# An ordering pass learns that VectorE and GpSimd take turns, and looks 500 instructions ahead instead of 300

## The chip, the cores and the metric

One core of one Trainium2 chip. The metric is device time in microseconds (us) from a launch's start to its end, as the median of several runs. The kernel before takes 2632.96 us (median of 3 runs, 2631.53 to 2633.64). Five engines work at once: TensorE (PE in the profile), VectorE (DVE), ScalarE (ACT), GpSimd (POOL), and SyncE (SP), which here issues every DMA. Each engine takes its instructions strictly in the order of its own queue; an instruction whose operands aren't ready holds up all those behind it on that engine, and no others, until someone waits for one of them.

## The reference

One layer of a bidirectional encoder over two sequences, one of 512 tokens and one of 1024, model width 1024, all in float32:

```python
h = rms_norm(x, n_pre_mix)
proj = h @ w_in                                   # 1024 x 6672
# Gated DeltaNet, 4 heads, forward and backward in time:
qkv = silu(centred_dwconv(qkv_g, conv_w))         # 5 taps
a_mat = where(strict, (k*beta) @ k.T * decay, 0)  # per chunk of 64
sol = triangular_solve(I + a_mat, [v*beta, k*beta*exp(cum)])
o_a = scan over chunks of (q, k, u, w, state)
# HGRN2, 4 heads, forward and backward: a linear recurrence with a decay per channel
o_b = gla_chunked(qh, kh, ih, logf)
merged = sigmoid(gate0) * (norm(o_a)*silu(z) @ w_br_gdn) + sigmoid(gate1) * (norm(o_b)*silu(g) @ w_br_hg)
x = x + rms_norm(merged @ w_out)
y = x + rms_norm((silu(h2 @ w_gate) * (h2 @ w_up)) @ w_down)   # d_ff 2816
```

## The kernel before, in words

The kernel is not written in the order in which it runs. `layer` calls its operations on a `Tape`, which only records them (about 19,400 operations, numbered in the order of recording); a simple planner, `Plan`, weaves the streams of work (`gdn_stream`, `hg_stream`, `pre_stream`, `dense_stream`, `p2_stream`) into that recording. Then `Tape.schedule` puts the operations into their final order and `Tape.emit` writes them out. Nearly every instruction therefore carries the one line number of `emit`: 564 before, 577 in the changed kernel, which has 13 lines more above it. In the profile groups are told apart by tile names instead: `la_a`, `ba_a`, `xa_a`, `da_a` and `xr_a` are large SBUF areas of 512-column buffers, `ha_a` holds the normalised activations, `wa_a` the split weights, `sm_a` and `sa_a` small tiles, `bank` is PSUM.

`schedule` is a list scheduler. It holds a clock for each engine and, for every operation, a duration (`o.dur`) and the time for which it occupies its engine (`o.occ`), both made up by `Tape.cost` from the operation's shape. Again and again it takes the engine that can start something first and, among the operations ready there, the one recorded earliest. What has not been recorded within `AHEAD` operations of the oldest unfinished one is not looked at. The durations are used for nothing but this order: if they are wrong, the queues are still correct, but an engine's next instruction may be one whose operands come late, while ready work stands behind it.

Where it matters here:

- **Matmuls in split precision.** A float32 product is made of three fp32r products; weights and activations are split into a high part (ScalarE) and a low part (VectorE, `split`, a `TENSOR_TENSOR` that writes `wa_a`, `ha_a` or `xr_a`). One projection tile of 128 output columns is 24 matmuls of 512 columns. These projections (`dense`, `gates`) are what TensorE does beside the recurrences.
- **A Gated DeltaNet head.** `gdn_in` makes keys and decays, `gdn_mix` makes the triangular matrices and sends them through DRAM (`u_sc`) to GpSimd, where `inverse` inverts all 32x32 diagonal blocks at once: 31 steps of a product and a subtraction, each needing the one before, on 8 to 256 columns, so 62 short GpSimd instructions in a row. The result goes through DRAM again (`w_sc`) and VectorE transposes it (`vtrans` in `merges`, the only `STREAM_TRANSPOSE` of 256 columns for the shorter sequence). Then `merges` puts the blocks together with 32x32 and 64x64 matmuls, and a scan of 4 or 8 steps follows. There are four heads for each sequence, so eight inverses; heads 0 to 3 of the shorter sequence come first.
- **HGRN2** (`hg_pre`) has subtractions of 256 columns on GpSimd (`level`) and much VectorE and ScalarE work.
- After both sequences come the branch and output projections (`p2_stream`) and the feed-forward part (`alone`, `both`, `down`), where GpSimd makes sums of weight quarters (`quarters`, `right`).

Before the change `cost` gives a GpSimd arithmetic instruction

```python
            d = 220 + 2.6 * n
```

nanoseconds for n columns, whatever VectorE does meanwhile, and lets the next GpSimd instruction that needs it start 30 ns later.

## Time and profile before

| | us |
|---|---|
| median of 3 runs | 2632.96 |
| the profiled execution's own time | 2635.52 |
| its span, first to last instruction | 2633.6 |
| TensorE busy | 2527.7 (96%) |
| VectorE busy | 1690.2 (64%) |
| ScalarE busy | 1279.6 (49%) |
| GpSimd busy | 700.3 (27%) |
| mean granted TensorE clock | 0.985 |

The span is that of the one profiled execution. In the views by stage each row gives a stretch's start and end, its length, the busy time of each engine with its count of instructions, the granted TensorE clock as a share of full speed, and the DMA traffic. Busy time of TensorE is time in which at least one matmul runs, fast or slow, so a low clock hides in it.

### The profile page before, as it was taken

What the parts mean: (1) busy time and instruction counts of PE and PEld (TensorE: products, weight loads), DVE (VectorE), ACT (ScalarE), POOL (GpSimd) and SP (SyncE); (2) the same over time, 40 slices, a digit from 0 to 9 for tenths busy, and PEclk for the clock granted to TensorE, in tenths of its full rate; (3) what the DMA queues carried; (4) which work ended last, traced back from release to release, by engine and by line L of the source; (5) the groups of instructions that cost most, each with busy time, mean ns of one, the idle gap of its engine ahead of it and who ended that gap; (6) DMA issues with size and microseconds to landing.
All of it is one profiled execution on the core that took longest, in us unless ns stands there. A gap on an engine that the chain in (4) does not pass through costs nothing.

```text
span 2633.6 us, 38737 instructions
## 1 busy us (share of the span) xinstructions
PE 2527.7 (96%) x14568; PEld 2079.6 (79%) x14568; DVE 1690.2 (64%) x2814; ACT 1279.6 (49%) x2178; POOL 700.3 (27%) x1011
## 2 busy tenths in 40 slices
PE   7898988999999999999999999999999999999998
PEld 6676767777778877877879888888878888888886
DVE  5666566775775575576584675465577878744558
ACT  5654556653553554554554354354444434533343
POOL 1523413123240150141110001111265766400014
PEclk9989999999999999999999999999999999999999
DMA  5332335131132122223166862455244455575445
GB/s 146 79 107 53 108 82 156 58 97 49 49 94 72 40 74 64 69 53 89 65 194 192 271 212 85 137 168 161 80 145 157 158 192 188 172 244 188 160 143 171
DMA packets 393450, 330.44 MB, mean 125 GB/s; under 512 B 55241, under 2 KB 328223, under 8 KB 393263
## 3 DMA queue, kind: packets, MB, share of 16 engines
q1 hardware_dynamic: 393263, 327.97, 40.8%
q8 instruction: 114, 1.87, 0.3%
q14 instruction: 73, 0.60, 0.1%
HBM read 251.44 MB, written 76.46 MB: 125 GB/s over the span
## 4 chain that ended last, share of the span: by engine, by line
PE 65%; DVE 6%; ACT 2%; issue 1%; POOL 0%; DMA 0%; DVEq 0%; ACTq 0%
PE bank L564 65%; DVE la_a L564 3%; DVE ba_a L564 2%; ACT la_a L564 1%; DVE wa_a L564 1%; DVE sa_a L564 0%; ACT ba_a L564 0%; ACT wa_a L564 0%; DVE sm_a L564 0%; ACT ha_a L564 0%; DVE ha_a L564 0%; DVE da_a L564 0%; POOL la_a L564 0%; DMA dram_g_sc<-ba_a 0%; ACT sa_a L564 0%
## 5 line engine op out<-in xcount | busy, mean ns | idle before, releaser
L564 PE MATMUL bank<-ha_a,wa_a 128*128 128x512 f32 x5496 | 1484.1, 411 | 20.0 <-DVE wa_a L564 16.5
L564 PEld LDWEIGHTS bank<-ha_a,wa_a 128*128 128x128 f32 x5496 | 1014.1, 191 | 229.2 <-DVE wa_a L564 25.8
L564 PE MATMUL bank<-xr_a,ha_a 128*128 128x512 f32 x1200 | 318.6, 395 | 1.7 <-DVE ha_a L564 1.7
L564 PE MATMUL bank<-xr_a 128*128 128x512 f32 x1386 | 315.7, 389 | 0.0
L564 PEld LDWEIGHTS bank<-xr_a 128*128 128x128 f32 x1386 | 260.1, 188 | 54.1
L564 POOL TENSOR_TENSOR ba_a<-ba_a 128x512 f32<-128x512 f32 (+1 forms) x129 | 168.9, 1317 | 488.1 <-DVE ba_a L564 286.5
L564 ACT ACTIVATE la_a<-la_a 128x512 f32<-128x512 f32 (+1 forms) x360 | 225.8, 644 | 93.5 <-DVE la_a L564 68.3
L564 PEld LDWEIGHTS bank<-xr_a,ha_a 128*128 128x128 f32 x1200 | 225.3, 188 | 55.9 <-DVE ha_a L564 2.1
L564 DVE TENSOR_TENSOR wa_a<-la_a,wa_a 128x1024 fp32r<-128x1024 f32 x110 | 134.4, 1235 | 130.0 <-PE bank L564 101.2
L564 DVE TENSOR_TENSOR wa_a<-ba_a,wa_a 128x1024 fp32r<-128x1024 f32 (+1 forms) x100 | 117.9, 1196 | 113.8 <-PE bank L564 83.0
L564 POOL TENSOR_TENSOR la_a<-la_a 128x256 f32<-128x256 f32 (+1 forms) x64 | 58.0, 924 | 451.0 <-DVE sa_a L564 296.9
L564 DVE TENSOR_TENSOR la_a<-la_a 128x512 f32<-128x512 f32 (+2 forms) x234 | 148.5, 652 | 13.1 <-ACT la_a L564 12.0
L564 ACT ACTIVATE ha_a<-ba_a 128x512 fp32r<-128x512 f32 x139 | 85.9, 627 | 142.1 <-PE bank L564 106.4
L564 ACT ACTIVATE wa_a<-la_a 128x1024 fp32r<-128x1024 f32 x110 | 115.1, 1054 | 75.0 <-PE bank L564 63.8
L564 PE MATMUL bank<-ha_a 128*128 128x512 f32 x480 | 149.4, 392 | 0.0
L564 PEld LDWEIGHTS bank<-wa_a,ha_a 128*128 128x128 f32 x1152 | 141.4, 192 | 1.2
L564 PE MATMUL bank<-wa_a,ha_a 128*128 128x256 f32 x1152 | 142.2, 283 | 0.0
L564 DVE TENSOR_TENSOR ha_a<-ba_a,ha_a 128x512 fp32r<-128x512 f32 x139 | 131.5, 953 | 8.9 <-ACT ha_a L564 8.0
L564 ACT ACTIVATE wa_a<-ba_a 128x1024 fp32r<-128x1024 f32 (+1 forms) x100 | 97.6, 993 | 70.3 <-PE bank L564 61.8
L564 PEld LDWEIGHTS bank<-la_a 128*32 128x32 f32 (+4 forms) x1778 | 101.7, 134 | 37.9 <-issue 13.5
L564 ACT COPY la_a<-bank 128x512 f32<-128x512 f32 (+1 forms) x133 | 70.4, 536 | 122.0 <-PE bank L564 121.6
L564 DVE TENSOR_TENSOR xr_a<-da_a,xr_a 128x1024 fp32r<-128x1024 f32 (+2 forms) x66 | 80.1, 1228 | 73.0 <-ACT xr_a L564 53.6
(183 smaller groups left out, 3460.0 us busy)
## 6 DMA issues: line engine op xcount, KB each, us to landing
la_a<-w_in SPq DMA_DIRECT2D x71, 512.0 KB, 5.4
ba_a<-w_ffn_gate SPq DMA_DIRECT2D x38, 512.0 KB, 3.9
ba_a<-w_ffn_up SPq DMA_DIRECT2D x37, 512.0 KB, 5.2
dram_a_sc<-xa_a SPq DMA_DIRECT2D x67, 256.0 KB, 2.2
ba_a<-w_in SPq DMA_DIRECT2D x33, 512.0 KB, 6.9
ba_a<-w_ffn_down SPq DMA_DIRECT2D x26, 512.0 KB, 4.1
da_a<-dram_a_sc SPq DMA_DIRECT2D x22, 512.0 KB, 8.1
dram_t_sc<-ba_a SPq DMA_DIRECT2D x20, 512.0 KB, 3.6
```

The source lines that it names most:

```text
L564: f(*[m(a) for a in o.args], **{k: m(a) for k, a in o.kw.items()})
```

## The change

Four things in `Tape`, all of them in what the scheduler believes; no operation is added, removed or computed otherwise.

1. **Turns.** An operation of VectorE whose operands all lie in SBUF, and one of GpSimd other than a memset, gets a `port`: 138 ns (65 more for each scalar operand) after its start it needs what the other engine may hold. In `schedule` such an operation that starts before the other engine's last one has ended is made longer by what is missing.
2. **GpSimd's own times** become those without that waiting: 192 + 1.87 n ns below 512 columns (2.15 n from there), and 78 instead of 30 ns to the next GpSimd instruction that needs the result.
3. **Smaller prices**: scan +10 ns, predicated copy and transposition +30 ns on VectorE, a ScalarE instruction with an accumulator, and a store of short rows to DRAM (600 ns of SyncE's queue instead of 380 or 450).
4. **`AHEAD`** is 500 instead of 300.

```diff
+    LAT = {("ACT", "PE"): 54, ("DVE", "PE"): 55, ("PE", "POOL"): 61, ("DVE", "POOL"): 86, ("ACT", "POOL"): 77,
+           ("POOL", "POOL"): 78}
...
-    AHEAD = 300
+    AHEAD = 500
...
             o.occ = 380.0 if rows < 512 else 450.0
+            if o.dur < 2000.0 and run < P:
+                o.occ = 600.0
...
-            if o.kw.get("accum_out") is not None:
-                d += 200
-            o.dur, o.occ = d, d - 95
+            o.dur, o.occ = d, d - (95 if o.kw.get("accum_out") is None else 0)
...
             ps = psum(out) or any(psum(i) for i in ins)
+            if not ps and m != "memset" and (m != "tensor_scalar" or n > 1):
+                o.port = 138 + 65 * len(scal)
             if m == "tensor_tensor_scan":
-                d = 145 + 1.98 * n
+                d = 155 + 1.98 * n
...
+            if m in ("copy_predicated", "transpose"):
+                d += 30
...
         else:
-            d = 220 + 2.6 * n
+            d = 192 + (1.87 if n < TB else 2.15) * n
+        if m != "memset":
+            o.port = 138
...
-            return 30 if a == b else self.LAT.get((b, a), 36)
+            return self.LAT.get((b, a), 30 if a == b else 36)
...
+        held = {"vector": 0.0, "gpsimd": 0.0}
...
+            if o.port:
+                w = max(0.0, held["gpsimd" if e == "vector" else "vector"] - t - o.port)
+                o.dur += w
+                o.occ += w
+                held[e] = t + o.dur
```

What this moves shows in the queues. The first place is VectorE's queue around the transposition of head 2's inverted blocks (the `STREAM_TRANSPOSE` of 256 columns; `wa_a` rows are low parts of weights, without which a projection's matmuls can't start). Before:

```order
L564 TENSOR_TENSOR la_a<-la_a 128x512
L564 TENSOR_TENSOR la_a<-bank_88,ba_a 128x512
L564 TENSOR_TENSOR la_a<-la_a 128x512 x3
L564 SCALAR_TENSOR_TENSOR la_a<-bank_90,ba_a 128x512
L564 TENSOR_TENSOR wa_a<-la_a,wa_a 128x1024 x2
L564 TENSOR_TENSOR ba_a<-bank_85,ba_a 128x512
L564 TENSOR_TENSOR la_a<-bank_85,la_a 128x512
L564 STREAM_TRANSPOSE la_a<-ba_a 128x256
```

With the change:

```order
L577 TENSOR_SCALAR ba_a<-ba_a,sa_a 128x512
L577 SCALAR_TENSOR_TENSOR ba_a<-sm_a,la_a 128x128 x4
L577 TENSOR_TENSOR la_a<-ba_a 128x512
L577 TENSOR_TENSOR wa_a<-la_a,wa_a 128x1024
L577 TENSOR_TENSOR wa_a<-ba_a,wa_a 128x1024
L577 TENSOR_TENSOR la_a<-la_a 128x512
L577 TENSOR_TENSOR la_a<-ba_a,la_a 128x512
L577 TENSOR_TENSOR la_a<-ba_a,la_a 128x8x32
L577 TENSOR_TENSOR la_a<-la_a 128x8x32
L577 TENSOR_SCALAR ba_a<-ba_a,sa_a 128x512
L577 STREAM_TRANSPOSE la_a<-la_a 128x256
```

Two more splits of weights and the HGRN2 work of the next head (scans, products, `8x32` parts of a level) now stand ahead of the transposition; before, they stood behind it.

The second place is GpSimd's queue in the middle of head 0's inverse, whose steps are the pairs that write `sm_a` and then `la_a` from `sm_a`. Before:

```order
L564 TENSOR_TENSOR sm_a<-la_a 128x66
L564 TENSOR_TENSOR la_a<-la_a,sm_a 128x3x22
L564 TENSOR_TENSOR sm_a<-la_a 128x63
L564 TENSOR_TENSOR la_a<-la_a,sm_a 128x3x21
L564 TENSOR_TENSOR sm_a<-la_a 128x60
L564 TENSOR_TENSOR la_a<-la_a,sm_a 128x3x20
L564 TENSOR_TENSOR sm_a<-la_a 128x76
L564 TENSOR_TENSOR la_a<-la_a,sm_a 128x4x19
```

With the change:

```order
L577 TENSOR_TENSOR sm_a<-la_a 128x60
L577 TENSOR_TENSOR la_a<-la_a 128x8x32
L577 TENSOR_TENSOR la_a<-la_a,sm_a 128x3x20
L577 TENSOR_TENSOR la_a<-la_a 128x8x32
L577 TENSOR_TENSOR sm_a<-la_a 128x76
L577 TENSOR_TENSOR la_a<-la_a 128x4x64
L577 TENSOR_TENSOR la_a<-la_a,sm_a 128x4x19
L577 TENSOR_TENSOR ba_a<-la_a 128x8x32
L577 TENSOR_TENSOR sm_a<-la_a 128x72
```

Eight HGRN2 level subtractions of 256 columns, which before came after the inverse, now alternate with its steps.

## The prediction

> **What bounds the kernel now.** I read the page first, then the busy time by stretches, then the waits, then GpSimd's and VectorE's timelines around TensorE's longest stops.

> ```profile
> span 2633.6 us, 38737 instructions
> PE 2527.7 (96%) x14568; PEld 2079.6 (79%) x14568; DVE 1690.2 (64%) x2814; ACT 1279.6 (49%) x2178; POOL 700.3 (27%) x1011
> PE 65%; DVE 6%; ACT 2%; issue 1%; POOL 0%; DMA 0%; DVEq 0%; ACTq 0%
> ```

> TensorE is the bound and the change leaves its matmuls as they are. What an order can win is TensorE's idle time, 2633.6 - 2527.7 = 105.9 us, and the time in which it runs at a lower clock. The stretches show where both lie (columns: stretch, length, busy TensorE, weight loads, VectorE, ScalarE, GpSimd, then granted clock, DMA share, GB/s):

> ```profile
> 108.60:113.20 4.60, 0.04 (x1) 0.04 (x1) 3.28 (x6) 3.54 (x6) 3.98 (x11) 0.93 0.09 35
> 113.20:124.40 11.20, 11.20 (x87) 8.88 (x87) 8.69 (x15) 3.96 (x7) 10.04 (x23) 0.88 0.15 37
> 124.40:127.60 3.20, 0.10 (x8) 0.09 (x11) 2.40 (x4) 2.33 (x5) 1.20 (x2) 0.79 0.89 245
> 127.60:150.30 22.70, 22.04 (x202) 16.21 (x202) 16.28 (x37) 9.09 (x16) 1.26 (x6) 0.50 0.13 30
> ...
> 205.80:215.40 9.60, 0.04 (x1) 0.00 (x0) 0.43 (x1) 0.59 (x1) 3.75 (x17) 0.62 0.08 14
> 215.40:218.60 3.20, 3.19 (x10) 2.47 (x11) 0.47 (x2) 0.59 (x1) 0.00 (x0) 0.53 0.44 76
> ...
> 331.80:340.50 8.70, 0.08 (x2) 0.05 (x1) 6.45 (x12) 1.90 (x4) 1.98 (x3) 0.65 0.57 151
> 340.50:344.90 4.40, 4.40 (x11) 3.49 (x12) 4.40 (x9) 2.65 (x4) 1.93 (x2) 0.52 0.01 4
> ...
> 442.00:449.10 7.10, 0.01 (x1) 0.01 (x1) 3.84 (x8) 5.37 (x14) 0.00 (x0) 0.86 0.96 271
> 449.10:454.00 4.90, 4.90 (x41) 4.07 (x42) 4.87 (x10) 2.47 (x8) 0.00 (x0) 0.51 0.55 161
> ...
> 604.90:611.20 6.30, 4.43 (x16) 3.35 (x16) 0.69 (x1) 2.39 (x5) 5.24 (x14) 0.73 0.00 0
> ...
> 650.00:1300.00 650.00, 626.92 (x4327) 513.69 (x4325) 416.51 (x820) 349.28 (x603) 150.93 (x303) 1.00 0.23 62
> 1300.00:1650.00 350.00, 343.64 (x2306) 304.42 (x2306) 222.56 (x397) 169.88 (x319) 18.85 (x15) 1.00 0.60 193
> ...
> 1920.00:2600.00 680.00, 679.68 (x2958) 555.49 (x2959) 463.34 (x549) 280.54 (x438) 265.06 (x175) 1.00 0.55 179
> 2600.00:2634.00 34.00, 21.70 (x96) 17.64 (x94) 23.10 (x41) 5.14 (x17) 14.64 (x10) 0.86 0.24 93
> ```

> Five stops of 4.56, 3.10, 9.56, 8.62 and 7.09 us, 32.9 in all, stand out, and behind each the clock is near half for a while. From 1920 us TensorE is full but for the tail; VectorE's and GpSimd's mutual waiting there costs nothing now.

> **Why it stops.** All five lie at the inverses of the first sequence's four heads. I take each head's time from the inverse's first step to VectorE's transposition of its result:

> ```profile
> 88.03 0.24 POOL L564 TENSOR_TENSOR sm_a<-la_a 128x31 f32<-128x31 f32 x1 [34.90 <-DMA la_a<-dram_u_sc]
> 177.37 1.16 POOL L564 TENSOR_TENSOR sm_a<-ba_a,la_a 128x31 f32<-128x31 f32 x1 [10.29 <-DMA la_a<-dram_u_sc]
> 294.01 0.78 POOL L564 TENSOR_TENSOR sm_a<-la_a 128x31 f32<-128x31 f32 x1 [24.11 <-DMA la_a<-dram_u_sc]
> 406.81 0.24 POOL L564 TENSOR_TENSOR sm_a<-la_a 128x31 f32<-128x31 f32 x1 [40.28 <-DMA la_a<-dram_u_sc]
> ```

> ```profile
> 130.74 0.44 DVE L564 STREAM_TRANSPOSE la_a<-la_a 128x256 f32<-128x256 f32 x1
> 218.13 0.45 DVE L564 STREAM_TRANSPOSE la_a<-la_a 128x256 f32<-128x256 f32 x1 [11.90 <-DMA la_a<-dram_w_sc]
> 334.02 0.45 DVE L564 STREAM_TRANSPOSE la_a<-ba_a 128x256 f32<-128x256 f32 x1 [13.30 <-DMA ba_a<-dram_w_sc]
> 448.02 0.44 DVE L564 STREAM_TRANSPOSE ba_a<-la_a 128x256 f32<-128x256 f32 x1
> ```

> That is 42.7, 40.8, 40.0 and 41.2 us. How many matmuls the order puts between the same two instructions is counted in the queues, which are written out in one common order. Before it is 130, 120, 127 and 126 of 512 columns, and 48, 10, 13 and 35 others; now 176, 160, 177 and 152, with 94, 46, 13 and 45. Prices:

> ```profile
> 1950.00:2000.00 50.00, 50.00 (x217) 40.49 (x216) 40.34 (x48) 19.23 (x32) 29.52 (x21) 1.00 0.57 184
> L564 PE MATMUL bank<-la_a 128*128 128x128 f32 x370 | 64.8, 276 | 3.0 <-ACT la_a L564 2.6 <-DVE la_a L564 0.2
> L564 PE MATMUL bank<-la_a,sm_a 128*128 128x512 f32 x80 | 42.1, 608 | 3.6 <-ACT la_a L564 3.6
> L564 PE MATMUL bank<-la_a 32*32 32x32 f32 x344 | 11.9, 201 | 1.0 <-DVE ba_a L564 0.5 <-DVE la_a L564 0.5
> ```

> 50 / 217 = 0.230 us for a 512-column fp32r matmul; 64.8 / 370 = 0.175 for a transposition and twice that for a plain float32 one of 128 columns (two passes), 1.05 for 512 columns, 0.07 for 32. With these, all of the program's matmuls would come to some 110 us more than TensorE was busy, so I scale all but the fp32r ones by 0.73, which makes the totals agree. The cover of the four heads before is 34.4, 30.7, 32.1 and 34.6 us, short of the measured times by 8.3, 10.1, 7.9 and 6.6, together 32.9: the very sum of the five stops. The order had put too little beside the inverse.

> The inverse is longer than planned because of blocking:

> ```profile
> 198.10 2.48 DVE L564 TENSOR_TENSOR wa_a<-la_a,wa_a 128x1024 fp32r<-128x1024 f32 x2 [0.55 <-PE bank L564]
> 199.58 1.20 POOL L564 TENSOR_TENSOR ba_a<-ba_a,sm_a 128x75 f32<-128x75 f32 x1
> 200.85 0.31 POOL L564 TENSOR_TENSOR sm_a<-ba_a,la_a 128x70 f32<-128x70 f32 x1
> 201.24 0.32 POOL L564 TENSOR_TENSOR ba_a<-ba_a,sm_a 128x70 f32<-128x70 f32 x1
> ```

> A step beside VectorE's split takes 1.20 us and ends with it; the next, alone, 0.31, with 0.39 from start to start. The old formula gave 75 columns 0.42 us either way.

> **The change, term by term** (us won against the span; the median, 2632.96, lies 0.6 below the span and stands for it).

> *The five stops: +29.9.* The new cover by the same prices is 52.1, 48.7, 43.6 and 41.9, against 42.7, 40.8, 40.0 and 41.2: room of 9.4, 7.9, 3.6 and 0.7. So all 32.9 would go, if the inverses stayed as long. Head 0's does not: the order now puts eight level subtractions and 58 instead of 24 SBUF-only VectorE instructions beside its steps.

> ```profile
> L564 POOL TENSOR_TENSOR la_a<-la_a 128x256 f32<-128x256 f32 x62 | 51.2, 843 | 154.1 <-DVE la_a L564 81.9 <-issue 22.6 <-ACT wa_a L564 21.3
> ```

> The last steps of head 0's and head 1's inverses before are

> ```profile
> 119.76 0.21 POOL L564 TENSOR_TENSOR la_a<-la_a,sm_a 128x8 f32<-128x8 f32 x1
> 210.39 0.21 POOL L564 TENSOR_TENSOR ba_a<-ba_a,sm_a 128x8 f32<-128x8 f32 x1
> ```

> Eight at 0.84 are 6.7. Of the VectorE instructions an additional one costs the inverse between 0 (it falls between steps) and 0.9 us (1.20 - 0.31); its 62 steps at 0.39 would be 24.2, it ran 31.9 with some 30 beside it, so about 0.25 each, 28 more are 7. That makes 42.7 + 13.7 = 56.4, less up to 3 (the transposition came 10.8 after the last step there, 7.5 at head 1), against 52.1: short by 1 to 4, I take 3. Extremes: 0 and 20. The other heads have 24, 25 and 49 such instructions, against 24, 22 and 42.

> *The clock: +11.3.* The missing share of the clock times the rows' lengths behind the stops, 1.3 + 11.4 + 1.5 + 2.1 + 2.4 = 18.7, is the most. The 11.4 is the 22.7 us at 0.50 over head 0's merges, whose small matmuls come as before and may hold the clock down by themselves: 0 to 11.4, I take half. One new low stretch for head 0's remaining stop, 1.7, goes off: 7.3 + 5.7 - 1.7. [...]

> *The second sequence: +5.3.* Its first head (604.9 us) is short in the same way by 1.9, and gets 183 instead of 163 fp32r matmuls. From 650 to 1300:

> ```profile
> PE bank L564 <- DVE la_a L564: 14.4, 13, 2.3
> ```

> Part of this is VectorE late behind GpSimd, which the order now allows for: 0 to 14.4, I take 3.4, half of three waits of the longest size.

> *Given back: -5.* The matmuls that now stand beside the inverses stood elsewhere. From the transposition to the scan's last state update the four heads have 23, 30, 25 and 36 us of them at unscaled prices, where they had 22, 40, 36 and 49. Head 0's took

> ```profile
> 157.96 0.66 DVE L564 SCALAR_TENSOR_TENSOR sm_a<-sm_a,bank 128x128 f32<-128x128 f32 x2 [0.27 <-PE bank L564]
> ```

> to 158.6, 27.9 from 130.74, much of it at half clock. At full clock I expect some 18, so that all four fit; at half they miss by 5, 0, 3 and 0. Between 0 and 20 (both middle heads missing ten, too) I take 5.

> *Nothing: the rest.* From 1300 us on TensorE's queue is nearly unchanged, and where VectorE and GpSimd shift, TensorE's work covers it (679.68 busy of 680). If that cover fell, one late split would cost what a split lasts, 1.2. The dearer row stores on SyncE change the order of a few DMAs; they hide beside the same matmuls. The larger `AHEAD` is what finds the additional matmuls; it has no cost of its own on the chip.

> Sum: 29.9 + 11.3 + 5.3 - 5 = 41.5, so 2591.5; I say 2592.

> **Rivals.**

> - *The stop moves into the merges* (2612). All four chains miss cover and run at half clock: the give-back is 20 and the clock's half of 11.4 stays too. For it: the halved cover of heads 1 and 2 above. Against it: head 0 had only 22 before, and TensorE was busy for 22.04 of the 22.70 us over its merges.
> - *Nothing gained* (2630). The lateness is the round trip of `w_sc` and not the steps, and each queue waits as before. For it: VectorE's 11.90 and 13.30 for that DMA. Against: only about 7.5 of each lie behind the inverse's last step, and as much is now covered.
> - *Slower* (2653). GpSimd's queue gets later work between the steps, so a mask (`AFFINE_SELECT`) whose row of decays hasn't landed stops the whole inverse. Two such masks stand inside head 0's inverse and two inside head 2's.

> ```profile
> POOL la_a L564 <- DMA la_a<-dram_cr_sc: 46.5, 9, 22.8
> ```

>   At 15 us each, inside the longest wait of 22.8, four cost 60: 2633 - 41 + 60. It decides from 10 us each. Against it: two masks stood inside head 0's inverse before, and the loads are issued 5 us of matmuls ahead now as then.
> - *More than expected* (2572): all of 32.9 and 18.7 and a third of the 650-to-1300 waits.

> **How the numbers follow.** The forecast (2578 to 2605) gets 0.60, the merges 0.14, nothing 0.08, slower 0.11, more 0.07. A change under 0.2% (5.3 us) can't be told from none: faster 0.81, same 0.08, slower 0.11. The range that leaves out 0.2 reaches from 2566 to 2629.

> **What would show it.** Right: TensorE's stops of 7 to 10 us at heads 1 to 3 are gone, those left lie at head 0's inverse; the granted clock from 100 to 470 us is nearly 1; inverses of 31 to 36 us for heads 1 to 3, over 42 for head 0. Wrong: a stop behind a mask on GpSimd, new stops over 3 us in the merges, or a time before 650 us that shrinks and comes back after it.

## The result, and the profile after

The changed kernel takes 2570.61 us (median of 4 runs, 2569.16 to 2577.28); the kernel before, on the same chip, 2633.30 (4 runs, 2631.53 to 2637.53). The ratio is 0.9765, with a 95% interval of 0.9744 to 0.9785: 62.7 us are won, where 41.5 were forecast, and the time lies below the forecast's 2578 to 2605. The profiled execution took 2570.76 us. The page of the changed kernel has its span, the busy times and the shares of the chain:

```profile
span 2569.0 us, 38723 instructions
PE 2513.3 (98%) x14568; PEld 2071.5 (81%) x14568; DVE 1693.8 (66%) x2814; ACT 1279.2 (50%) x2178; POOL 721.3 (28%) x1011
PE 85%; DVE 8%; DMA 3%; ACT 2%; issue 1%; POOL 1%; SPq 0%; DVEq 0%; ACTq 0%; POOLq 0%
```

TensorE's idle time fell from 105.9 to 55.7 us (2569.0 - 2513.3), and the same 14568 matmuls took 14.4 us less busy time. That is the clock: by the traces' clock records, time at half clock fell from 80.4 to 39.9 us. Where both came from is seen when each run is cut where the last state update of the shorter sequence's head 3 ends: at 497 us before, at 444 now. Two rows of the stretches before,

```profile
24.00:497.00 473.00, 431.31 (x2689) 343.75 (x2690) 306.02 (x594) 263.77 (x462) 141.92 (x337) 0.94 0.34 92
497.00:2634.00 2137.00, 2087.33 (x11848) 1729.22 (x11846) 1366.29 (x2154) 997.75 (x1671) 550.97 (x646) 0.99 0.42 132
```

and the two of the changed kernel:

```profile
24.00:444.00 420.00, 410.73 (x2691) 331.42 (x2691) 310.19 (x600) 260.72 (x464) 156.37 (x344) 1.00 0.39 106
444.00:2569.00 2125.00, 2093.63 (x11846) 1733.63 (x11845) 1366.70 (x2146) 999.61 (x1669) 556.89 (x635) 0.99 0.43 132
```

The counts of matmuls agree within two, so the rows can be subtracted. The first stage is 53.0 us shorter: TensorE's idle time in it fell from 41.7 to 9.3 us (32.4 less), its busy time by 20.6 at a clock that rose from 0.94 to 1.00. The rest is 12 us shorter: idle time fell from 49.7 to 31.4 (18.3 less), while busy time grew by 6.3: time at half clock rose there from 22.4 to 39.9 us.

What TensorE waited for from 24 to 470 us, before and now (waited for: total us, times, longest):

```profile
PE bank L564 <- DVE la_a L564: 14.5, 8, 7.1
PE bank L564 <- DVE wa_a L564: 13.3, 3, 8.6
PE bank L564 <- ACT ba_a L564: 9.6, 1, 9.6
```

```profile
PE bank L577 <- DVE la_a L577: 4.0, 8, 1.2
PE bank L577 <- ACT ba_a L577: 2.1, 3, 1.2
PE bank L577 <- DVE ba_a L577: 1.6, 4, 0.5
```

None of the five stops is left; the longest is 1.2 us. The wait for splits of weights (`wa_a`) is gone as a group. GpSimd's timeline gives the inverse's first step of the four heads, VectorE's the transposition:

```profile
85.40 0.24 POOL L577 TENSOR_TENSOR sm_a<-la_a 128x31 f32<-128x31 f32 x1 [36.38 <-DMA la_a<-dram_u_sc]
151.83 0.55 POOL L577 TENSOR_TENSOR sm_a<-ba_a,la_a 128x31 f32<-128x31 f32 x1 [18.06 <-DMA la_a<-dram_u_sc]
262.72 0.46 POOL L577 TENSOR_TENSOR sm_a<-ba_a 128x31 f32<-128x31 f32 x1 [45.80 <-DMA ba_a<-dram_u_sc]
369.85 0.24 POOL L577 TENSOR_TENSOR sm_a<-la_a 128x31 f32<-128x31 f32 x1 [56.32 <-DMA la_a<-dram_u_sc]
```

```profile
140.93 0.45 DVE L577 STREAM_TRANSPOSE ba_a<-la_a 128x256 f32<-128x256 f32 x1 [1.99 <-DMA la_a<-dram_w_sc]
199.18 0.43 DVE L577 STREAM_TRANSPOSE ba_a<-la_a 128x256 f32<-128x256 f32 x1
306.45 0.43 DVE L577 STREAM_TRANSPOSE la_a<-la_a 128x256 f32<-128x256 f32 x1
409.97 0.44 DVE L577 STREAM_TRANSPOSE ba_a<-ba_a 128x256 f32<-128x256 f32 x1
```

That is 55.5, 47.4, 43.7 and 40.1 us. The way is longer than before at three heads of four (42.7, 40.8, 40.0, 41.2), and TensorE no longer waits for it. Only at head 0 does VectorE still wait for the load, 1.99 us.

### The profile page after: what moved, and what is told of

The parts are those of the page before. It is cut to its first block, busy times and chain, and to the rows that moved or that the text cites. A ratio compares the mean times of both kernels' runs of the same rounds, so it can differ in the third digit from the quotient of the medians.

```text
span 2569.0 us, 38723 instructions
## 1 busy us (share of the span) xinstructions
PE 2513.3 (98%) x14568; PEld 2071.5 (81%) x14568; DVE 1693.8 (66%) x2814; ACT 1279.2 (50%) x2178; POOL 721.3 (28%) x1011
## 3 DMA queue, kind: packets, MB, share of 16 engines
q1 hardware_dynamic: 393263, 327.97, 42.1%
q8 instruction: 114, 1.87, 0.3%
## 4 chain that ended last, share of the span: by engine, by line
PE 85%; DVE 8%; DMA 3%; ACT 2%; issue 1%; POOL 1%; SPq 0%; DVEq 0%; ACTq 0%; POOLq 0%
PE bank L577 85%; DVE la_a L577 4%; DVE ba_a L577 2%; DVE wa_a L577 1%; ACT la_a L577 1%; DMA la_a<-dram_cr_sc 1%; ACT ba_a L577 1%; DVE sa_a L577 1%; DMA la_a<-dram_u_sc 0%; SPq L577 0%; POOL sm_a L577 0%; DMA dram_g_sc<-la_a 0%; DVE ha_a L577 0%; ACT wa_a L577 0%; DVE sm_a L577 0%
## 5 line engine op out<-in xcount | busy, mean ns | idle before, releaser
L577 PE MATMUL bank<-ha_a,wa_a 128*128 128x512 f32 x5496 | 1465.6, 408 | 5.9 <-ACT wa_a L577 1.8
L577 POOL TENSOR_TENSOR ba_a<-ba_a 128x512 f32<-128x512 f32 (+2 forms) x120 | 169.6, 1419 | 559.0 <-DVE sa_a L577 306.2
L577 ACT ACTIVATE la_a<-la_a 128x512 f32<-128x512 f32 (+1 forms) x314 | 200.7, 651 | 77.4 <-DVE la_a L577 50.0
L577 DVE TENSOR_TENSOR wa_a<-la_a,wa_a 128x1024 fp32r<-128x1024 f32 x114 | 140.6, 1243 | 121.7 <-PE bank L577 90.1
L577 DVE TENSOR_TENSOR la_a<-la_a 128x512 f32<-128x512 f32 (+2 forms) x218 | 142.2, 671 | 14.0 <-ACT la_a L577 13.0
L577 ACT ACTIVATE ba_a<-ba_a 128x512 f32<-128x512 f32 x175 | 109.3, 629 | 34.5 <-DVE ba_a L577 27.7
L577 PEld LDWEIGHTS bank<-la_a 128*32 128x32 f32 (+4 forms) x1690 | 93.7, 133 | 33.0 <-issue 11.1
```

The costliest lines, as they stand in the source:

```text
L577: f(*[m(a) for a in o.args], **{k: m(a) for k, a in o.kw.items()})
```

## The experiments

Twelve kernels, all computing the same. The expectations use letters for the theories:

- **C**, cover: matmuls counted in the order between an inverse's first step and VectorE's transposition, against the time this takes (the prediction's theory).
- **A**: looking 500 operations ahead is what does it. **S**: any other order would.
- **E**: the plan must know when the inverse ends. **T**: it must know which instruction waits for which, in both directions.
- **Q**: SyncE's queue, held at the inverse's store. **V**: VectorE alone is late.
- **F**: filling the small stops of the merges wins them and the clock. **D**: the low clock comes from the density of small matmuls and stays.

Diffs are against the changed kernel where it says so, else against the kernel before. Ratios are to the kernel before, measured beside each.

### Without the turns

Against the changed kernel:

```diff
-            if o.port:
+            if False:
```

> The changed kernel without part 1: no operation is made longer for the other engine; GpSimd's times alone, the smaller prices and 500 operations ahead stay. Theory C (cover): what counts is how many microseconds of matmuls the order puts between an inverse's first step and VectorE's transposition, against the time that this takes (42.7, 40.8, 40.0, 41.2 in the shorter sequence, 46.6 and three times about 48.5 in the longer one, measured in the kernel before). Counted as in the prediction, this order has 36.1, 32.3, 32.3, 31.1 and 40.0, 39.0, 46.7, 46.7: short by 6.6, 8.5, 7.7, 10.1 and 6.6, 9.8, 1.8, 1.8, together 53 where before it was 33 and 5. So the stops stay, two new ones of 7 to 10 us come at the longer sequence's first two heads, and the time is 2633 + 15 = 2648, 2640 to 2665: slower than before. Theory A (looking ahead is what finds the filler): most of the gain stays, 2575 to 2590. Theory S (any other order would do, the old one was unlucky): the five stops are gone without a reason in the counts, anything from 2570 to 2600.

Measured: 2666.91 us, ratio 1.0124 (1.0105 to 1.0143). Slower than before, 2 us above C's range; A and S are out. The stage that holds the five stops is as long as before (475.5 us, see the table below); the 32 us are lost in the rest, where time at half clock rose from 22.4 to 78.6 us, which C doesn't count. TensorE's stops over 2 us in the first stage are 6.0 and 8.5, 4.9, 2.5 and 4.9, and 6.9 for heads 0 to 3, together 33.6 where the counts say 32.9; the longer sequence's first head has one of 6.3 where they say 6.6, while the one of 9.8 at its second didn't come. Head by head the counts are worse than in sum: 14.5 at head 0 where they say 6.6. They also take head 0's time from the kernel before, 42.7 us, and here it was 52.7. The new prices without the turns make the plan's inverse too short by as much as the old formula did, and the larger `AHEAD` doesn't help.

### 300 operations ahead

Against the changed kernel:

```diff
-    AHEAD = 500
+    AHEAD = 300
```

> The changed kernel with 300 instead of 500 operations ahead; the turns and all prices stay. Theory C (cover): the counts are 35.6, 45.8, 41.5, 43.5 and 49.9, 50.0, 50.0, 50.0: only head 0 is short, by 7.1 (42.7 against 35.6). One stop of about 7 us at head 0's inverse, a low clock over its merges behind it (up to the 11.4 us of the kernel before), nothing at heads 1 to 3: 2571 + 7 + 4 to 11, so 2582 to 2589. Theory A (looking ahead): most of the gain is gone, 2615 to 2633. Theory S (any other order): no statement on where a stop is left.

Measured: 2594.94 us, ratio 0.9853 (0.9836 to 0.9870), 24 us behind the changed kernel and 6 above C's range. TensorE's timeline:

```profile
125.62 1.22 PE L577 MATMUL bank<-la_a,sm_a 128*128 128x512 f32 x1 [7.11 <-ACT la_a L577]
```

The one long stop of the first stage is at head 0, 7.11 us where the count says 7.1. The turns and prices win 38 of the 63 us without the larger window. Of the other 24, 14 lie in the first stage, with the filler at head 0, as C said; 9 lie in the rest, about which C says nothing and where TensorE has two stops of 3.5 us, at 1402 and 1497 us.

### Only 500 operations ahead

```diff
-    AHEAD = 300
+    AHEAD = 500
```

> The kernel before with 500 instead of 300 operations ahead and nothing else. Theory C (cover): the counts are 39.0, 32.8, 32.3, 32.4 and 42.9, 47.7, 47.3, 47.3: short by 3.7, 8.0, 7.7, 8.8, together 28 of the 33 before, and by 3.7 and some 1 each in the longer sequence. The stops stay, a little shorter at head 0: 2633 - 5, so 2622 to 2635. Theory A (looking ahead): most of the gain comes, 2575 to 2595. Theory S (any other order): the stops are gone though the counts say they stay.

Measured: 2642.12 us, ratio 1.0040 (1.0023 to 1.0057): slightly slower, 7 us beyond C's range, and A is out for good. The stops over 2 us at heads 0 to 3 are 6.0 and 6.5, 5.1, 2.9 and 3.5, and 4.6, together 28.7 where the counts say 28.2, again with too much of it at head 0. The first stage is as long as before (473 us), the rest 8 us longer.

### Late loads

The turns replaced by one constant, with 500 ahead:

```diff
+            if vo is not None and "w_sc" in ins[0].tensor.name:
+                o.dur += 9000.0
```

> The kernel before with 500 operations ahead and one new price: the load of the inverted blocks (from w_sc) is planned 9 us longer than any other load. No turns, GpSimd's old formula, no smaller prices. Theory C (cover): the counts are 48.0, 46.4, 42.4, 41.4 and 50.5, 50.2, 50.5, 50.5, at or above the measured times everywhere, so all stops of 3 us and more are gone and the time is that of the changed kernel within some 10 us: 2565 to 2580. The turns would then be worth what one constant in the right place is worth. Theory T (turns: the order must know which VectorE instruction blocks which GpSimd instruction, or the small waits of the longer sequence and the merges stay): 2585 to 2600, since only the five stops and their clock, 30 to 50 us, can go. Theory A (looking ahead alone): the same time as 500 ahead with nothing else.

Measured: 2633.59 us, ratio 0.9999 (0.9981 to 1.0016). C, which had the sum of the stops right to a microsecond three times, is wrong here by more than 50 us: measured by the times of the kernel before, the cover is there, and nothing is won. Head 0's time from first step to transposition grew to 62.7 us, beyond its cover of 48.0. T's range is missed as well, and only A comes near, for a reason of its own. In the profile (its run, 2624.6, is the fastest of ten) TensorE stops for 5.6 us at 109 and 5.1 us at 139, between these two instructions of head 0. The second stop, in the timelines of SyncE's queue, ScalarE and TensorE:

```profile
132.06 2.64 SPq L566 DMA_DIRECT2D dram_w_sc<-la_a  x4
136.12 1.82 SPq L566 DMA_DIRECT2D la_a<-dram_w_sc  x4
137.98 0.45 SPq L566 DMA_DIRECT2D la_a<-w_in  x1
...
142.09 1.06 ACT L566 ACTIVATE wa_a<-la_a 128x1024 fp32r<-128x1024 f32 x1 [5.86 <-DMA la_a<-w_in]
...
143.62 0.57 ACT L566 COPY la_a<-bank 128x512 f32<-128x512 f32 x1
...
144.25 0.58 PE L566 MATMUL bank<-ba_a,la_a 128*128 128x128 f32 x1 [5.12 <-ACT la_a L566]
```

The store of the inverse's result goes out at 132.06, when the inverse ends. Behind it in SyncE's queue stand the loads of the result and a load of weights (`w_in`), which therefore starts at 137.98. ScalarE waits 5.86 us for these weights, and a copy that TensorE needs stands behind that. The constant had moved what follows the loads, but the store kept the place of a too early inverse. The cover counts only matmuls; it doesn't see whether their weights are in time.

### One direction of the turns

Against the changed kernel, behind the line that works out `w`; the second kernel has `"vector"` in the place of `"gpsimd"`:

```diff
+                w = w if e == "gpsimd" else 0.0
```

> The changed kernel with turns in one direction: only GpSimd's operations are made longer when VectorE holds the operands, never VectorE's. Theory E (the inverse's end): what the order has to know is when the inverse ends, since its store on SyncE, the loads behind that store and the transposition are placed by it; VectorE's own lengthening is small change. The counts of cover are 48.7, 45.1, 45.9, 39.8 and 45.2, 46.3, 46.7, 46.7, so at most 1.4 short at head 3 and 1 to 3 in the longer sequence: 2570 to 2585. Theory T (both directions matter, since VectorE's splits come late beside GpSimd's subtractions): 2590 to 2615.

Measured: 2616.27 us, ratio 0.9928 (0.9908 to 0.9949). E is out, and T's range is missed by 1 us.

> The changed kernel with turns in the other direction alone: only VectorE's operations are made longer, never GpSimd's. Theory E (the inverse's end) and the cover counts (36.5, 32.3, 31.7, 31.7 and 39.7, 44.1, 46.7, 46.7) both have all stops stay, as without any turns (2667): 2645 to 2670. Theory T: half of the difference between no turns and both, so about 2620.

Measured: 2638.15 us, ratio 1.0020 (1.0006 to 1.0034), below E's range and 18 us above T's figure. From no turns (2666.9), GpSimd's side alone wins 51 us, VectorE's alone 29, both together 96, 16 more than their sum; why more than the sum isn't shown. What the first kernel lacks shows in its timelines of VectorE and TensorE:

```profile
101.57 1.53 DVE L578 TENSOR_TENSOR_SCAN la_a<-sm_a,la_a 128x128 f32<-128x128 f32 x4
...
104.57 2.30 DVE L578 TENSOR_TENSOR_SCAN la_a<-sm_a,la_a 128x128 f32<-128x128 f32 x4
...
111.47 1.34 DVE L578 TENSOR_TENSOR wa_a<-la_a,wa_a 128x1024 fp32r<-128x1024 f32 x1
...
112.86 0.50 PE L578 MATMUL bank<-ha_a,wa_a 128*128 128x512 f32 x1 [3.87 <-DVE wa_a L578]
```

VectorE works without a pause here, and is late all the same: four scans take 2.30 us beside GpSimd's subtractions, where four of the same size just ahead took 1.53. The split that TensorE needs comes at 111.47, and TensorE has stopped for 3.87 us. These rows show VectorE's side; the prediction's step of 1.20 us beside a split, 0.31 alone, shows GpSimd's.

### A long inverse

```diff
-    AHEAD = 300
+    AHEAD = 500
...
-            d = 220 + 2.6 * n
+            d = 360 + 2.6 * n
```

> The kernel before with 500 operations ahead and 360 instead of 220 ns in GpSimd's old formula: 62 steps are planned 8.7 us longer, whatever VectorE does; no turns, no smaller prices. Other than with the late loads, the inverse's last step, and so its store on SyncE, is planned 9 us later too, and not the load alone. Theory E (the inverse's end): cover 50.1, 44.1, 42.0, 41.2 and 51.5, 51.4, 51.2, 51.2, and SyncE isn't held at the store: 2570 to 2590, near the changed kernel without any turns in the plan. Theory T (the plan must know which instruction waits for which): some of the stops stay, 2600 to 2635, as with the late loads.

Measured: 2610.29 us, ratio 0.9903 (0.9882 to 0.9923): inside T's range, outside E's. A constant for each step does a little more than GpSimd's side of the turns (2616.3), and 40 us less than both sides.

### A late store

```diff
-    AHEAD = 300
+    AHEAD = 500
...
-                        enable(s, fin + lat(e, s.eng))
+                        late = s.meth == "dma_start" and "w_sc" in s.args[0].tensor.name
+                        enable(s, fin + lat(e, s.eng) + (9000.0 if late else 0.0))
```

> The kernel before with 500 operations ahead and 9 us put on the way from the inverse's last step to the store of its result into w_sc (with the late loads they stood behind that store). No turns, no other price. Cover 48.0, 41.6, 42.2, 41.9 and 51.9, 51.6, 51.9, 51.9, about that of the late loads (48.0, 46.4, 42.4, 41.4), which gained nothing. Theory Q (SyncE's queue: with the late loads the store stood in SyncE's queue where a shorter inverse would have ended, held the weight loads behind it, and TensorE waited for weights): the store now stands where the inverse really ends, so the 5 us stops that waited for a load are gone, and the time is that of the long inverse, 2600 to 2615. Theory V (VectorE late beside GpSimd was all that the late loads missed, which a late store doesn't mend either): 2625 to 2640.

Measured: 2615.80 us, ratio 0.9929 (0.9910 to 0.9947): at the edge of Q (0.8 above), 9 below V. The same 9 us, put ahead of the store and not behind it, are worth 18 us; so much of the late loads' failure was SyncE's queue. Two long stops are left in the first stage, 6.0 and 4.3 us. The second, in the timelines of GpSimd, VectorE and TensorE:

```profile
289.75 0.63 POOL L565 TENSOR_SCALAR_AFFINE_SELECT la_a<-la_a 128x512 f32<-128x512 f32 x1
...
290.41 0.79 DVE L565 TENSOR_TENSOR la_a<-la_a,sm_a 128x512 f32<-128x512 f32 x1 [3.92 <-POOL la_a L565]
...
294.26 0.80 PE L565 MATMUL bank<-ha_a,wa_a 128*128 128x512 f32 x1 [4.28 <-DVE wa_a L565]
```

A mask stands between the inverse's steps. The first steps ahead of it last 0.33 to 1.10 us on 28 to 31 columns, where the old formula has 0.3, so it comes late; VectorE waits 3.92 us for it and TensorE 4.28 for the split behind. The constant was put at the inverse's end and can't move what stands in its middle. The long inverse, which has the additional time at each step, shows no such stop: only its stop at head 0, 4.3 us, is above 2 us in the first stage.

### The prices

Two kernels against the changed one. The first has GpSimd's old formula and latency under the turns:

```diff
-           ("POOL", "POOL"): 78}
...
-            d = 192 + (1.87 if n < TB else 2.15) * n
+            d = 220 + 2.6 * n
```

> The changed kernel with GpSimd's old formula (220 + 2.6 n, 30 ns to the next one) under the turns, so that the inverse is planned with blocking on top of a formula that already held some of it. Cover 52.4, 49.8, 50.0, 43.5 and 51.9, 49.5, 50.2, 50.2. Theory E: too late costs nothing as long as the filler is there, so as fast as the changed kernel within 8 us, 2565 to 2580. If GpSimd's times alone matter by themselves (too late a plan moves the matmuls that the merges would need): 2585 to 2600.

Measured: 2572.08 us, ratio 0.9757 (0.9739 to 0.9775). The same as the changed kernel: under the turns, GpSimd's new times bring nothing. The second has the old smaller prices (part 3 of the change undone):

```diff
-            if o.dur < 2000.0 and run < P:
-                o.occ = 600.0
...
+            if o.kw.get("accum_out") is not None:
+                d += 200
+            o.dur, o.occ = d, d - 95
...
-            if m in ("copy_predicated", "transpose"):
-                d += 30
```

> The changed kernel without part 3, the smaller prices (scans, predicated copies and transpositions on VectorE, ScalarE's accumulator, row stores on SyncE); turns, GpSimd's own times and 500 operations ahead stay. The prediction has the smaller prices at nothing. Cover 52.5, 51.3, 43.4, 40.3 and 48.0, 53.7, 49.8, 49.8, at most 0.9 short, at head 3. If the prediction is right: 2565 to 2580, as the changed kernel. If the row stores' place in SyncE's queue or the inverse's transposition (30 ns) matter by what is queued behind them: 2585 or more.

Measured: 2578.87 us, ratio 0.9793 (0.9765 to 0.9821). 8 us behind the changed kernel; the two intervals overlap, so a small part of the gain may lie here, or none.

### The merges

Against the changed kernel, 700 in one kernel and 1500 in the other. `form` is set for the small float32 matmuls alone:

```diff
-            o.dur = o.occ + 165
+            o.dur = o.occ + 165 + (0 if o.form is None else 700)
```

> The changed kernel with 700 ns more in the plan from a small float32 matmul (32 or 64 columns) to whoever waits for it; nothing else. It is meant for the stops of 0.5 to 0.8 us inside the merges, four for each head of the longer sequence, and for the half clock behind them (three stretches of about 10 us in the changed kernel). Theory F (filler): the order puts 512-column matmuls in these gaps, some 6 of the 13 us of idle time between 24 us and 1300 us outside the first sequence go, and with fewer small matmuls in a row the low clock too, up to 14: 2552 to 2568. Theory D (the low clock goes by the density of small matmuls and comes anyway, shifted): 2565 to 2572.

> The same with 1500 instead of 700 ns. Theory F (filler): as with 700 or a little better, 2550 to 2568, unless the merges' chain itself becomes what TensorE waits for (a stop of some us at the scan behind it), then 2570 to 2580. Theory D (density): 2565 to 2575.

Measured: 2547.92 us, ratio 0.9673 (0.9659 to 0.9688), and 2544.61 us, ratio 0.9660 (0.9645 to 0.9675). Both are faster than both kernels, the second by 26 us than the changed one, and beyond F's ranges on the fast side. The page of the second:

```profile
span 2544.3 us, 38738 instructions
PE 2499.1 (98%) x14568; PEld 2062.6 (81%) x14568; DVE 1696.8 (67%) x2814; ACT 1278.7 (50%) x2178; POOL 718.3 (28%) x1011
```

Against the changed kernel TensorE's idle time fell from 55.7 to 45.2 us and its busy time by 14.2. What it waited for in the longer sequence, in the changed kernel (444 to 1263 us) and in the second of these (445 to 1243):

```profile
PE bank L577 <- DVE la_a L577: 6.3, 9, 1.6
PE bank L577 <- DVE ba_a L577: 5.6, 10, 0.8
PE bank L577 <- ACT la_a L577: 0.8, 1, 0.8
```

```profile
PE bank L577 <- DVE la_a L577: 1.2, 3, 0.6
PE bank L577 <- ACT sm_a L577: 1.0, 1, 1.0
```

The small stops of the merges are filled, and the clock with them. D is out. Whether the stops or the unbroken runs of small matmuls hold the clock down wasn't told apart: the filler ends both.

### All of them in one table

The first stage is from 24 us to the end of head 3's last state update, the rest from there to the span's end, both from the profiled run of each kernel.

| kernel | median us | first stage | rest |
|---|---|---|---|
| before | 2633.3 | 473.0 | 2136.6 |
| no turns | 2666.9 | 475.5 | 2168.6 |
| only 500 ahead | 2642.1 | 473.2 | 2144.3 |
| only VectorE waits | 2638.2 | 469.8 | 2143.8 |
| late loads | 2633.6 | 455.6 | 2143.3 |
| only GpSimd waits | 2616.3 | 438.7 | 2151.9 |
| late store | 2615.8 | 446.4 | 2144.2 |
| long inverse | 2610.3 | 437.4 | 2145.8 |
| 300 ahead | 2594.9 | 433.8 | 2133.9 |
| no smaller prices | 2578.9 | 424.2 | 2129.0 |
| old GpSimd times | 2572.1 | 422.9 | 2121.7 |
| the changed kernel | 2570.6 | 420.1 | 2124.9 |
| merges 700 | 2547.9 | 418.2 | 2104.1 |
| merges 1500 | 2544.6 | 420.7 | 2099.6 |

With GpSimd's side alone, or with a constant in the right place, 27 to 36 of the first stage's 53 us are won; the rest of the program is then 8 to 15 us longer than before. That is the clock: in the rest of these three kernels TensorE's idle time is 45 to 48 us where it was 49, and its time at half clock 42 to 54 us where it was 22. Only kernels with both sides of the turns have a rest that is shorter than before; in the changed kernel its idle time is 31 us.

## Why the prediction was right, and where its sizes were off

**The mechanism** was right: TensorE stopped because the order put too little work beside an inverse that is longer than planned, and the turns mend it. With three other orders (no turns, 300 ahead, only 500 ahead) the same count gave the sum of the stops to within a microsecond, though single heads only to 9. Part of that is luck, since the count was set against the times of the kernel before. Set against each kernel's own times from first step to transposition, it is short by 42.0, 13.4 and 33.9 us where the stops are 33.6, 7.1 and 28.7: it tells which order has long stops, and their size only roughly. It was incomplete in one point: it takes cover to be a matter of matmuls alone. The late loads had the cover by that count and gained nothing, since the weights for it were loaded behind the inverse's store. The turns put every step, mask, store and split at its own time, and so get this right without the count's saying so.

**The five stops, +29.9.** Measured: the stops (32.9) are gone, and head 0's inverse, forecast as 56.4 us from first step to transposition, took 55.5. The 3 us that were to remain there did so as four stops of 1.2, 0.4, 0.5 and 0.5, together 2.6. Net 30.3: the term is right. (In its sum for head 0 a number is off: from 24 to 58 VectorE instructions are 34 more, not 28; at its 0.25 each the 56.4 would be 57.9.) The inverses themselves, from first to last step, took 47.6, 34.9, 34.6 and 30.8 us, close to the 31 to 36, and over 42 at head 0, that it named as signs. With 2 us of smaller waits the stage's idle time fell by 32.4.

**The clock, +11.3: mis-sized.** In the first stage it gave the 20.6 us of busy time shown above, more than the 18.7 that it took as the most: a stretch of 3.41 us at half clock from 464.2 us stands in none of the rows that were added up. The step that failed is that half of the 11.4 us over head 0's merges would stay, "whose small matmuls come as before and may hold the clock down by themselves", and with it the new low stretch of 1.7. No run shows that 1.7 for a remaining stop: behind the four left at head 0, 2.6 us together, the clock stayed at 1.00. The clock is 1.00 over the whole stage, so these small matmuls don't hold it down by themselves at head 0. Where a stop stands ahead of them they are slow again: behind stops of 8.5 us (no turns), 6.5 (only 500 ahead) and 2.7 (only VectorE waits) there are 23.9, 23.9 and 17.1 us at half clock.

**The second sequence, +5.3: mis-sized.** It was priced by half of three waits. The rows from 444 us on have 18.3 us less idle time, more than three times as much: the three waits of some 2.2 us fell to between 0.6 and 0.8, four of 1.1 to 1.3 went, and the first head's inverse no longer runs short. Against it stands what the prediction hadn't, 6.3 us more busy time, with 39.9 us at half clock where there were 22.4 (below). Net 12.

**Given back, -5: mis-sized.** Nothing was given back. From the transposition to the last state update the four heads took 27.9, 40.3, 38.2 and 49.0 us before, and 20.8, 28.2, 23.2 and 34.2 now, 49 less in all, and no wait above 1.2 us came into them: where matmuls moved away the stretch became shorter with them. The prediction had expected 18 at head 0.

**Nothing: the rest.** GpSimd's own times: nothing under the turns. Without the turns, the new times and smaller prices together cost 25 us (2666.9 against 2642.1). The smaller prices under the turns: 0 to 8. `AHEAD`: it "finds the additional matmuls", as said, for 24 us together with the turns, but it isn't free: without them it costs some 9 us (2642.1 against 2633.3).

Summed by what was measured: 30.3 and 2 of other idle time, 20.6 and 12 make 65, against the span's 64.6. Of the cases it is "more than expected" (2572), which had a chance of 0.07, by just its mechanism: all the stops, all their clock, part of the later waits. The other rivals didn't come: the merges are shorter, and no mask stops TensorE in the changed kernel, though a mask did so in the kernel with the late store.

## What to carry to other kernels

In an order made from planned durations, a chain that is planned too short costs the wait at its end and all that was placed by that end: stores, the loads queued behind them, splits and masks. So correct the instructions that are really longer, in both directions where two engines block each other (here 1.20 us against 0.31 for a GpSimd step, 2.30 against 1.53 for four VectorE scans), before looking further ahead; one constant, at the chain's end or for each of its steps, won between nothing and little more than a third. Then look at the granted clock again: filling stops of 0.5 to 0.8 us in the merges was worth another 26 us.

## What the runs showed of the hardware that wasn't expected

```profile
959.06:962.47 3.41, 2.42 (x97) 2.16 (x98) 1.43 (x4) 3.30 (x5) 0.00 (x0) 1.00 0.02 5
962.47:972.71 10.24, 9.45 (x47) 7.35 (x47) 4.62 (x10) 1.26 (x2) 1.27 (x2) 0.50 0.43 110
```

Behind 1.0 us of idle time in 3.41, split over two stops amid matmuls of 32 columns, 10.24 us at half clock follow, in which TensorE was busy for 9.45. Idle time alone doesn't decide it. The same two stops stand in the merges of the longer sequence's second head, at 756.3 and 757.8 us, where a border, counted from 587 us in steps of 3.41 us, lies between them (757.67 us), and the clock stayed full (1.00). It also stayed full in the kernel before behind 3.41 us from 979.55 us in which TensorE was busy for only 1.49, amid matmuls of 128 and 512 columns. That small matmuls on both sides of a stop make the difference is likely from these rows, but no run tests it. In the profiles of all the kernels here there are 118 low stretches between start and tail, and each lasts 1 to 8 times 3.41 us (59 of them once, 29 twice, 23 three times). In the rows above the clock fell behind 3.41 us with 2.42 us busy, and stayed low over three times 3.41 us busy for nine tenths. The prediction's 22.7 us at 0.50 lie in one of seven times 3.41, 23.89 us from 126.24 us. That the stretches can be had back is shown: with the merges filled, the longer sequence runs at full clock.

```profile
629.00:1243.00 614.00, 612.19 (x4322) 498.88 (x4321) 407.13 (x771) 344.44 (x592) 149.50 (x296) 1.00 0.27 76
```

TensorE is busy for 612.19 of 614 us in this row of the kernel with 1500 ns.
